# Latent attention's up-projections advanced piece by piece between halves of the convolution products, on a ring of five prepared and two raw weight tiles

## The chip, the cores and the metric

The kernel runs on one core of one Trainium2 chip. The metric is device time in microseconds (us) of one execution. TensorE (PE) multiplies matrices, with its weight loads (PEld) shown apart; VectorE (DVE), ScalarE (ACT) and GpSimd (POOL) work on tiles; SyncE (SP) issues DMA transfers. Each engine runs its own instructions in a fixed order and waits on semaphores for the others.

## The reference

Two blocks follow one another on 528 (16 meta and 512 real) and then 512 tokens of width 1024, all in float32. Block 1, one layer, computes

```
u, q, k, v, g_ssm, g_att = split(rmsnorm(h) @ w_in)
mixed = sigmoid(g_ssm) * (s5_mixer(u) @ w_ssm_out) + sigmoid(g_att) * (diff_attention(q, k, v) @ w_att_out)
h = h + mixed @ w_o
h = h + conv_glu_ffn(rmsnorm(h))
```

Block 2, two layers, projects a normed input to four branches, joins them with `w_out` and adds a normed result:

```
(a_val, a_glu, a_gate, b_q, b_f, b_i, b_gate, c_xbc, c_dt, c_z, d_cq, d_ckv, d_kr, d_gate) = split(rms_norm(x) @ w_in)
y_a = conformer_conv_branch(...)     # 31 taps along the tokens, layer norm, product
y_b = hgrn2_branch(...)              # gated recurrence in chunks of 64
y_c = ssd_branch(c_xbc, ...)         # 4 taps along the tokens, state space scan in chunks
y_d = mla_branch(d_cq, d_ckv, ...)   # latent attention
x = x + rms_norm(concat(y_a, y_b, y_c, y_d) @ w_out)
```

The latent attention `mla_branch` is what the change moves. From a normed query latent of 256 and a key-value latent of 128 columns it makes, by up-projections, the queries (64 plain and 32 rotated columns for each of 4 heads), the keys and the values:

```
q = (rms_norm(cq) @ qb_w);  q_rope = q_rope * cos + swapped(q_rope) * sin
k_nope, v = split(rms_norm(ckv) @ kvb_w)
o = softmax(mask(q k^T * 96 ** -0.5)) v        # 4 blocks of 128 queries x 4 heads
return o * silu(gate)
```

## The kernel before

**Products.** Every float32 product is made of three products of rounded parts, hi x hi, lo x hi and hi x lo (lines 466 to 468 of `mm3`), so a weight tile exists as `wh` (rounded) and `wl` (the rest). A product of one output tile of 128 columns over 1024 inputs and 512 tokens is 8 x 3 = 24 matmuls in one PSUM bank. PSUM has three banks for products (`pj`), two each for `sA` and `sB` (small products, scores, transposes) and one `so` (attention output). A product tile of a given bank can start only when the last result in that bank was read.

**Weights.** 197 tiles of 128 x 1024 stream from one tensor. `_fetch` (line 424 on) loads a raw tile `wr` by SP's queue, ScalarE copies it to `wh` (line 439), copies minus `wh` to `wl` (line 441), and GpSimd issues a DMA that adds the raw weights into `wl` (line 442). The first four tiles take `wl` from a VectorE subtraction instead (line 444). `weights(key)` hands out the next tile and keeps four fetched; the rings hold three raw and four prepared tiles.

**Order.** The code of block 2 is written as generators ("tasks"): `pump()` advances each task by one step, and `fm()`, the function for one product tile, pumps in the middle of its product and behind it, so a task's small products stand between halves of large ones. The tile framework's scheduler then sets each engine's order. In a layer of block 2 the products run b_f, b_q, kvm (the key-value latent and two small groups), d_cq (the query latent), b_i, a_glu and a_val; the gated recurrence (`hgrn_task`, its products at lines 345 and 1723) and, from the first a_val product on (read by VectorE's line 2273), the conformer convolution (`conf_conv`, 31 taps by line 1505 on VectorE) run beside them. Then `mla_proj` (line 2078) is called in one go: two query products, the rope products `pr` and `px` with VectorE's line 2098 (cos) and 2099 (sin) reading them, the key products, the value products (lines 2119 to 2121). It pumps the other tasks five times between its parts. Behind it come the six `c_xbc` products with `ssd_conv` between them, then c_z and the gates. The attention itself, `mla_attend`, is a task of 19 steps (score, line 2141; transposes, line 492; output, line 2169) and a closing part: gate multiplication by GpSimd, transposes, and the branch's parts 6 and 7 of the joining product `out2`.

**The end of a layer.** `out2` makes 8 output tiles, five over 512 tokens and three over two halves of 256; then a norm, the residual, and `lead` (lines 2358 to 2361): the first products of the next layer, of which the first weight tiles are held until all are done.

**Small pool.** 70 units of 128 x 528 serve all intermediate tiles; `S5_STARTS` sets at which pump count each of three groups of S5 work begins.

The pieces that the steps below follow:

```
w0 = self.weights(("sm", (l, 0)))
w1 = self.weights(("sm", (l, 1)))
self.spawn(self.mla_attend(l, *self.mla_proj(w0, w1)))
for g in range(2):
    for i in (g, 2 + g, 4 + g):
        self.xbc[i] = self.ssd_conv(l, i, self.fm(l, "c_xbc", i))
```

Of the kernel before, what the change touches and what calls it, by code (L numbers as in the profile page):

```python
# [8 lines left out]
F32 = mybir.dt.float32  # L9
F32R = mybir.dt.float32r  # L10
I32 = mybir.dt.int32
AF = mybir.ActivationFunctionType
ALU = mybir.AluOpType
# [6 lines left out]
GW = 1024  # L20
# [13 lines left out]
class Layout:  # L34
    def __init__(self):
        self.off = {}
        self.n = 0
# [273 lines left out]


class Build:
    NU = 70
    S5_STARTS = (8, 16, 24)
    HP = 300
    GLU_AT = 9

    def __init__(self, ctx, tc, ap, dbg=None):
        self.tc = tc  # L320
        self.nc = nc = tc.nc
        self.ap = ap
        self.dbg = dbg or {}
        self.vl, self.cl = layouts()
        ec = ctx.enter_context
        self.cp = ec(tc.tile_pool(name="cp", bufs=1))
        self.up = ec(tc.tile_pool(name="up", bufs=1))
        self.wp = ec(tc.tile_pool(name="wp", bufs=4))
        self.sp = ec(tc.tile_pool(name="sp", bufs=4))
        self.dp = ec(tc.tile_pool(name="dp", bufs=1, space=bass.MemoryType.DRAM))  # L330
        self.pp = ec(tc.tile_pool(name="pp", bufs=1, space=bass.MemoryType.PSUM))
        self.free_units = list(range(self.NU))
        self.owner = {}
        self.nid = 0
        self.worder = weight_order()
        self.wq = []
        self.tasks = []
        self.wnext = 0
# [81 lines left out]
    def _fetch(self, ahead=HP):  # L420
        nc = self.nc
        i = self.wnext
        self.wnext += 1
        kind, a = self.worder[i]
        n = GW
        if kind == "dn":
            n = (a[1] - a[0]) * 128
        elif kind == "pw" or kind == "sm" and a[1] == 0:
            n = 512
        with self.tc.high_priority(offset=ahead):  # L430
            raw = self.wp.tile([128, GW], F32, tag="wr", name=self.uid("wr"), bufs=3)
            h = self.wp.tile([128, GW], F32R, tag="wh", name=self.uid("wh"))
            l = self.wp.tile([128, GW], F32R, tag="wl", name=self.uid("wl"))
            cs = [slice(0, n)] if i else [slice(0, 512), slice(512, GW)]
            for c in cs:
                nc.sync.dma_start(out=raw[:, c], in_=self.ap["wst"][i, :, c])
            acc = self.lacc(i, kind, a)
            for c in cs:
                nc.scalar.activation(out=h[:, c], in_=raw[:, c], func=AF.Copy)  # L439
                if acc:  # L440
                    nc.scalar.activation(out=l[:, c], in_=h.bitcast(F32)[:, c], func=AF.Copy, scale=-1.0)  # L441
                    nc.gpsimd.dma_start(out=l[:, c], in_=self.ap["wst"][i, :, c], accum_op=ALU.add)  # L442
                else:
                    nc.vector.tensor_tensor(out=l[:, c], in0=raw[:, c], in1=h.bitcast(F32)[:, c], op=ALU.subtract)
        self.wq.append((self.worder[i], h, l))

# [1 line left out]
        return i >= 4  # L448

    def weights(self, key):  # L450
        while len(self.wq) < 4 and self.wnext < len(self.worder):
            self._fetch()
        k, h, l = self.wq.pop(0)
        assert k == key, (k, key)
        return h, l
# [794 lines left out]
    def block1(self):  # L1250
# [17 lines left out]
        def tick():  # L1268
            self.step += 1
            if self.step in self.S5_STARTS:  # L1270
                self.spawn(s5[self.S5_STARTS.index(self.step) + 1])
            self.pump()
# [802 lines left out]
            yield  # L2075
        self.free(*cq)

    def mla_proj(self, w0, w1):
        nc = self.nc
        V, G = nc.vector, nc.gpsimd  # L2080
        mm = nc.tensor.matmul
        SC = 96.0 ** -0.5
        ks, xk, xq = self.mks, self.xk, self.xq
        qs = [self.unit(F32, "mq") for _ in range(4)]
        for t in range(2):
            p = self.pj()
            self.mm3(p, w0[0], w0[1], t * 128, 128, 2, xq, slice(0, S), kstep=256)
            for hh in range(2):
                nc.scalar.activation(out=qs[t * 2 + hh][:64, :S], in_=p[hh * 64:hh * 64 + 64], func=AF.Copy, scale=SC)
            self.pump()  # L2090
        pr = self.pj()
        self.mm3(pr, w1[0], w1[1], 0, 128, 2, xq, slice(0, S))
        px = self.pj()
        self.mm3(px, w1[0], w1[1], 256, 128, 2, xq, slice(0, S))
        for x in xq:
            self.free(*x)
        ro, t = self.unit(), self.unit()
        V.tensor_tensor(out=ro[:, :S], in0=pr, in1=self.cosT, op=ALU.mult)  # L2098
        V.tensor_tensor(out=t[:, :S], in0=px, in1=self.sinT, op=ALU.mult)
        G.tensor_tensor(out=ro[:, :S], in0=ro[:, :S], in1=t[:, :S], op=ALU.add)  # L2100
        for h in range(4):
            nc.scalar.activation(out=qs[h][64:96, :S], in_=ro[h * 32:h * 32 + 32, :S], func=AF.Copy, scale=SC)
        self.free(ro, t)
        self.pump()
        for t in range(2):
            p = self.pj()
            self.mm3(p, w1[0], w1[1], 512 + t * 128, 128, 1, [xk], slice(0, S))
            nc.scalar.activation(out=ks[t * 2][:64, :S], in_=p[0:64], func=AF.Copy)
            nc.scalar.activation(out=ks[t * 2 + 1][:64, :S], in_=p[64:128], func=AF.Copy)
        self.pump()  # L2110
        vt = []
        for t in range(2):
            p = self.pj()
            for u in range(2):
                j = t * 2 + u
                o = p[:, u * 256:u * 256 + 256]
                sl = slice(j * 128, j * 128 + 128)
                wh, wl = w1[0][:, 768:1024], w1[1][:, 768:1024]
                mm(out=o, lhsT=xk[0][:, sl], rhs=wh, start=True, stop=False)
                mm(out=o, lhsT=xk[0][:, sl], rhs=wl, start=False, stop=False)  # L2120
                mm(out=o, lhsT=xk[1][:, sl], rhs=wh, start=False, stop=True)
            v = self.unit(F32, "mv")
            nc.scalar.activation(out=v[:, :S], in_=p, func=AF.Copy)
            vt.append(v)
        self.free(*xk)
        self.pump()
        return qs, ks, vt

    def mla_attend(self, l, qs, ks, vt):
        nc = self.nc  # L2130
# [73 lines left out]
    def layer(self, l):  # L2204
        nc = self.nc
# [71 lines left out]
                self.spawn(self.conf_conv(l, ths))  # L2277
            self.pump()
        self.spawn(self.conf_rest(l))
        w0 = self.weights(("sm", (l, 0)))  # L2280
        w1 = self.weights(("sm", (l, 1)))
        self.spawn(self.mla_attend(l, *self.mla_proj(w0, w1)))
        for g in range(2):
            for i in (g, 2 + g, 4 + g):
                self.xbc[i] = self.ssd_conv(l, i, self.fm(l, "c_xbc", i))
# [65 lines left out]
        for hs in H2:  # L2351
            for a in range(2):
                for k in range(8):
                    xh, xl = self.xn[k]
                    c = slice(k * 128, k * 128 + 128)
# [112 lines left out]
```

## Time and profile before

| | |
|---|---|
| median of 3 runs | 1389.48 us (1389.32 to 1390.44) |
| profiled execution | 1390.1 us, span 1388.3 us |
| PE busy | 1337.1 us, 96% |
| PEld, DVE, ACT, POOL busy | 87%, 58%, 56%, 34% |
| mean granted clock of TensorE | 0.982 of full speed |
| weights and other reads | 209.33 MB, 154 GB/s over the span |

The table is of one execution. Block 1 ends near 800 us; layer 0 of block 2 runs from there to about 1065 us, the turn from layer 0 to layer 1 lies between 1065 and 1112 us, and layer 1 ends the span. A stretch in which PE is busy all the time at granted clock 1.00 can't give time without fewer matmuls; a stretch with idle PE or a lower clock can. So the views of waits and of single stretches say more here than the shares of the span.

### The profile page before, as it was taken

What the parts mean: (1) busy time and instruction counts of PE and PEld (TensorE: products, weight loads), DVE (VectorE), ACT (ScalarE), POOL (GpSimd) and SP (SyncE); (2) the same over time, 40 slices, a digit from 0 to 9 for tenths busy, and PEclk for the clock granted to TensorE, in tenths of its full rate; (3) what the DMA queues carried; (4) which work ended last, traced back from release to release, by engine and by line L of the source; (5) the groups of instructions that cost most, each with busy time, mean ns of one, the idle gap of its engine ahead of it and who ended that gap; (6) DMA issues with size and microseconds to landing.
All of it is one profiled execution on the core that took longest, in us unless ns stands there. A gap on an engine that the chain in (4) does not pass through costs nothing.

```text
span 1388.3 us, 22901 instructions
## 1 busy us (share of the span) xinstructions
PE 1337.1 (96%) x8778; PEld 1201.4 (87%) x8778; DVE 805.0 (58%) x1951; ACT 777.9 (56%) x1217; POOL 471.5 (34%) x557
## 2 busy tenths in 40 slices
PE   8899999999999999999999989899998799899998
PEld 8898898999999988998898888779987798689986
DVE  8969776423533322332233485998633696998623
ACT  7565555654555443444445856665657666664653
POOL 4557731113332221221124443632212453632210
PEclk9999999999999999999999999999999889999999
DMA  8855555598888888888887956464468456474483
GB/s 271 219 120 115 116 118 130 128 227 185 182 195 185 186 187 192 185 186 191 186 180 159 208 118 153 106 150 107 96 138 202 101 127 145 91 164 102 92 175 91
DMA packets 72254, 215.54 MB, mean 155 GB/s; under 512 B 10705, under 2 KB 17361, under 8 KB 72145
## 3 DMA queue, kind: packets, MB, share of 16 engines
q0 software_dynamic: 27648, 98.58, 42.7%
q1 hardware_dynamic: 43488, 113.80, 25.3%
q10 hardware_dynamic: 1008, 1.70, 0.4%
q8 instruction: 69, 1.13, 0.3%
q14 instruction: 41, 0.33, 0.1%
HBM read 209.33 MB, written 4.72 MB: 154 GB/s over the span
## 4 chain that ended last, share of the span: by engine, by line
PE 78%; DVE 14%; ACT 1%; issue 1%; DMA 1%; POOL 0%; DVEq 0%; ACTq 0%
PE pj L466 17%; PE pj L468 17%; PE pj L467 17%; DVE cc L1505 3%; PE pj L1482 3%; PE pj L1481 3%; PE pj L1483 3%; PE sB L492 2%; PE sB L2141 1%; PE so L2169 1%; PE pj L2326 1%; PE pj L2324 1%; PE pj L2325 1%; DMA wl<-in_wst 1%; PE sB L1174 1%
## 5 line engine op out<-in xcount | busy, mean ns | idle before, releaser
L466 PE MATMUL pj<-xh,wh 128*128 128x512 f32 (+4 forms) x1700 | 556.4, 328 | 7.4 <-DVE u L2098 4.0
L467 PE MATMUL pj<-xl,wh 128*128 128x512 f32 (+4 forms) x1700 | 554.0, 326 | 0.0
L468 PE MATMUL pj<-xh,wl 128*128 128x512 f32 (+4 forms) x1700 | 554.0, 326 | 0.0
L439 ACT ACTIVATE wh<-wr 128x1024 fp32r<-128x1024 f32 (+2 forms) x197 | 203.8, 1036 | 353.1 <-PE pj L467 298.0
L442 POOL DMA_DIRECT2D wl<-in_wst x192 | 167.6, 873 | 560.2 <-ACT wl L441 544.8
L466 PEld LDWEIGHTS pj<-xh,wh 128*128 128x128 f32 x1700 | 321.9, 189 | 37.2 <-DVE u L2098 4.9
L467 PEld LDWEIGHTS pj<-xl,wh 128*128 128x128 f32 x1700 | 321.8, 189 | 26.6 <-issue 0.2
L468 PEld LDWEIGHTS pj<-xh,wl 128*128 128x128 f32 x1700 | 321.4, 189 | 26.9 <-issue 0.4
L441 ACT ACTIVATE wl<-wh 128x1024 fp32r<-128x1024 f32 (+2 forms) x192 | 198.6, 1036 | 2.7
L1481 PE MATMUL pj<-wh,xh 128*128 128x256 f32 x384 | 114.5, 298 | 3.2 <-DVE u L1595 3.1
L1482 PE MATMUL pj<-wl,xh 128*128 128x256 f32 x384 | 112.6, 293 | 4.1 <-DMA wl<-in_wst 4.1
L1483 PE MATMUL pj<-wh,xl 128*128 128x256 f32 x384 | 112.6, 293 | 0.0
L1481 PEld LDWEIGHTS pj<-wh,xh 128*128 128x128 f32 x384 | 75.5, 197 | 6.0 <-issue 5.8
L1482 PEld LDWEIGHTS pj<-wl,xh 128*128 128x128 f32 x384 | 75.3, 196 | 5.9 <-DMA wl<-in_wst 4.4
L1483 PEld LDWEIGHTS pj<-wh,xl 128*128 128x128 f32 x384 | 75.4, 196 | 1.0 <-issue 1.0
L1505 DVE SCALAR_TENSOR_TENSOR cc<-u,aw,cc 128x496 f32<-128x496 f32 (+17 forms) x84 | 73.2, 876 | 0.3
L1405 DVE TENSOR_TENSOR hT<-hT,pj 128x512 f32<-128x512 f32 x24 | 16.4, 687 | 88.3 <-PE pj L468 88.3
L1384 DVE TENSOR_TENSOR u<-pj,nsR 128x258 f32<-128x258 f32 (+1 forms) x44 | 18.6, 425 | 76.2 <-PE pj L468 68.9
L1390 DVE TENSOR_TENSOR u<-u,pj 128x512 f32<-128x512 f32 x22 | 15.2, 689 | 64.8 <-PE pj L468 60.4
L1512 POOL TENSOR_TENSOR ce<-ce,u 128x489 f32<-128x489 f32 (+7 forms) x32 | 47.4, 1482 | 10.7 <-ACT u L1511 9.6
L529 POOL TENSOR_TENSOR nsA<-nsA,u 128x514 f32<-128x514 f32 (+3 forms) x23 | 29.5, 1281 | 48.5 <-ACT u L528 36.5
L488 DVE SCALAR_TENSOR_TENSOR xl<-hT,vec,xh 128x256 fp32r<-128x256 f32 (+3 forms) x40 | 28.3, 723 | 18.8 <-ACT xh L487 18.8
(626 smaller groups left out, 2356.8 us busy)
## 6 DMA issues: line engine op xcount, KB each, us to landing
wr<-in_wst SPq DMA_DIRECT2D x183, 512.0 KB, 3.9
wl<-in_wst POOLq DMA_DIRECT2D x180, 512.0 KB, 6.0
hT<-in_xT SPq DMA_DIRECT2D x16, 264.0 KB, 5.7
wr<-in_wst SPq DMA_DIRECT2D x8, 384.0 KB, 3.1
wl<-in_wst POOLq DMA_DIRECT2D x8, 384.0 KB, 5.4
wr<-in_wst SPq DMA_DIRECT2D x6, 256.0 KB, 4.6
UD<-us SPq DMA_DIRECT2D x4, 264.0 KB, 6.9
U<-UD SPq DMA_DIRECT2D x16, 66.0 KB, 5.5
```

Of the source, the lines that this page charges most:

```text
L439: nc.scalar.activation(out=h[:, c], in_=raw[:, c], func=AF.Copy)
L441: nc.scalar.activation(out=l[:, c], in_=h.bitcast(F32)[:, c], func=AF.Copy, scale=-1.0)
L442: nc.gpsimd.dma_start(out=l[:, c], in_=self.ap["wst"][i, :, c], accum_op=ALU.add)
L466: mm(out=out, lhsT=a, rhs=xh[:, sl], start=k == 0, stop=False)
L467: mm(out=out, lhsT=a, rhs=xl[:, sl], start=False, stop=False)
L468: mm(out=out, lhsT=b, rhs=xh[:, sl], start=False, stop=k == nk - 1)
L529: eng.tensor_tensor(out=st["A"][:, hs], in0=st["A"][:, hs], in1=s[:, hs], op=ALU.add)
L1481: mm(out=o, lhsT=xh[:, sl], rhs=h, start=k == 0, stop=False)
L1482: mm(out=o, lhsT=xh[:, sl], rhs=lo, start=False, stop=False)
L1483: mm(out=o, lhsT=xl[:, sl], rhs=h, start=False, stop=k == 7)
L1505: V.scalar_tensor_tensor(out=c[:, o:S], in0=th[:, :S - o], scalar=aw[:, i, 30 - o:31 - o], in1=c[:, o:S], op0=ALU.mult, op1=ALU.add)
L1512: G.tensor_tensor(out=e[:, k:S], in0=e[:, k:S], in1=t[:, :S - k], op=ALU.add)
```

## The change

Four edits. (1) The pool of units shrinks from 70 to 68, and the third S5 group starts at count 28 instead of 24. (2) The prepared ring grows from four to five tiles, the raw ring shrinks from three to two, and five tiles are kept fetched. (3) `_fetch` makes `wl` from the raw tile by itself, before `wh`, and issues the adding DMA before `wh` is made. (4) `mla_proj` becomes a generator that fetches its own weights and yields eight times; a new task `mla_task` runs it and then the attention, and is put first among the tasks, so its parts now stand between halves of the `c_xbc` products.

```diff
-    NU = 70
-    S5_STARTS = (8, 16, 24)
+    NU = 68
+    S5_STARTS = (8, 16, 28)
...
-        self.wp = ec(tc.tile_pool(name="wp", bufs=4))
+        self.wp = ec(tc.tile_pool(name="wp", bufs=5))
...
-            raw = self.wp.tile([128, GW], F32, tag="wr", name=self.uid("wr"), bufs=3)
+            raw = self.wp.tile([128, GW], F32, tag="wr", name=self.uid("wr"), bufs=2)
...
             for c in cs:
+                if acc:
+                    nc.scalar.activation(out=l[:, c], in_=raw[:, c], func=AF.Copy, scale=-1.0)
+                    nc.gpsimd.dma_start(out=l[:, c], in_=self.ap["wst"][i, :, c], accum_op=ALU.add)
                 nc.scalar.activation(out=h[:, c], in_=raw[:, c], func=AF.Copy)
-                if acc:
-                    nc.scalar.activation(out=l[:, c], in_=h.bitcast(F32)[:, c], func=AF.Copy, scale=-1.0)
-                    nc.gpsimd.dma_start(out=l[:, c], in_=self.ap["wst"][i, :, c], accum_op=ALU.add)
-                else:
+                if not acc:
                     nc.vector.tensor_tensor(out=l[:, c], in0=raw[:, c], in1=h.bitcast(F32)[:, c], op=ALU.subtract)
...
-        while len(self.wq) < 4 and self.wnext < len(self.worder):
+        while len(self.wq) < 5 and self.wnext < len(self.worder):
...
-    def mla_proj(self, w0, w1):
+    def mla_proj(self, l):
...
+        w0, w1 = (self.weights(("sm", (l, i))) for i in range(2))
...
-            self.pump()
+            yield
         pr = self.pj()
         self.mm3(pr, w1[0], w1[1], 0, 128, 2, xq, slice(0, S))
+        yield
         px = self.pj()
...
+    def mla_task(self, l):
+        qkv = yield from self.mla_proj(l)
+        yield from self.mla_attend(l, *qkv)
...
-        w0 = self.weights(("sm", (l, 0)))
-        w1 = self.weights(("sm", (l, 1)))
-        self.spawn(self.mla_attend(l, *self.mla_proj(w0, w1)))
+        self.tasks.insert(0, self.mla_task(l))
+        self.pump()
```

By the change the rope reads of VectorE are lines 2100 and 2101, the score is line 2149, the output line 2177, the value products lines 2121 to 2123, and the copies and the adding DMA of `_fetch` are lines 442 (`wh`), 440 (`wl`) and 441.

**First place: PE in layer 0, the up-projections.** Before, `pj_9511` and `pj_9518` are the rope products, `pj_9539` and `pj_9545` the keys, `pj_9589` the first values, and `pj_9616` the first `c_xbc` product. Left-out rows are the other matmuls of the same tiles.

```order
L466 MATMUL pj_9511<-xh_9049,wh_9317 128x512
...
L466 MATMUL pj_9518<-xh_9049,wh_9317 128x512
...
L1791 MATMUL sA_9494<-u_9041,u_9466 128x128 x2
...
L466 MATMUL pj_9539<-xh_8851,wh_9317 128x512
...
L466 MATMUL pj_9545<-xh_8851,wh_9317 128x512
...
L2119 MATMUL pj_9589<-wh_9317,xh_8851 128x256
...
L466 MATMUL pj_9616<-xh_8015,wh_9385 128x512
```

In the changed kernel `pj_9559` and `pj_9591` are the rope products, `pj_9666` and `pj_9702` the keys, and `pj_9578` and `pj_9689` are `c_xbc` products.

```order
L466 MATMUL pj_9559<-xh_9056,wh_9231 128x512
...
L466 MATMUL pj_9578<-xh_8022,wh_9392 128x512
...
L466 MATMUL pj_9591<-xh_9056,wh_9231 128x512
...
L466 MATMUL pj_9578<-xh_8036,wh_9392 128x512
...
L466 MATMUL pj_9666<-xh_8858,wh_9231 128x512
...
L1912 MATMUL sA_9674<-bd_8830,s_8827 128x512
L466 MATMUL pj_9689<-xh_8022,wh_9447 128x512
...
L466 MATMUL pj_9702<-xh_8858,wh_9231 128x512
```

Before, the rope products stand side by side and the keys follow 6 matmuls behind; now 19 matmuls of a `c_xbc` product stand between the two rope products, its last 5 between the second rope product and the first key product, and 20 of the next `c_xbc` product between the two key products.

**Second place: ScalarE at the turn from layer 0 to layer 1.** Line 498 and 499 make the last part of the norm factors; the tiles `wr_11469`, `wr_11476` and `wr_11706` are the first three weights behind `lead`. Before:

```order
L499 ACTIVATE nsR_11158<-nsR_11158 128x256
L439 ACTIVATE wh_11470<-wr_11469 128x1024
L439 ACTIVATE wh_11477<-wr_11476 128x1024
L439 ACTIVATE wh_11707<-wr_11706 128x1024
L498 ACTIVATE nsR_11158<-sB_11634,eps_129 128x256
L441 ACTIVATE wl_11471<-wh_11470 128x1024
L441 ACTIVATE wl_11478<-wh_11477 128x1024
L441 ACTIVATE wl_11708<-wh_11707 128x1024
L499 ACTIVATE nsR_11158<-nsR_11158 128x256
```

In the changed kernel the first of the three was prepared earlier; the second and third are `wr_11476` and `wr_11483`, and `wr_11713` is the fourth.

```order
L499 ACTIVATE nsR_11165<-nsR_11165 128x256
L442 ACTIVATE wh_11477<-wr_11476 128x1024
L440 ACTIVATE wl_11478<-wr_11476 128x1024
L442 ACTIVATE wh_11484<-wr_11483 128x1024
L440 ACTIVATE wl_11485<-wr_11483 128x1024
L498 ACTIVATE nsR_11165<-sB_11641,eps_129 128x256
L499 ACTIVATE nsR_11165<-nsR_11165 128x256
L440 ACTIVATE wl_11715<-wr_11713 128x1024
```

Six copies of weights stand ahead of the last norm factors before, four in the changed kernel.

**Third place: ScalarE in the first 35 us.** `wr_169` and `wr_176` are the first two weights whose `wl` is made by an adding DMA, line 710 is a sine with its table load, line 498 begins the norm factors. Before:

```order
L439 ACTIVATE wh_170<-wr_169 128x1024
L441 ACTIVATE wl_171<-wh_170 128x1024
L439 ACTIVATE wh_177<-wr_176 128x1024
L441 ACTIVATE wl_178<-wh_177 128x1024
L710 ACT_TABLE_LOAD
L710 ACTIVATE s_cs<-s_cs 128x32
L402 ACT_TABLE_LOAD
```

In the changed kernel:

```order
L710 ACT_TABLE_LOAD
L710 ACTIVATE s_cs<-s_cs 128x32
L402 ACT_TABLE_LOAD
L440 ACTIVATE wl_171<-wr_169 128x1024
L442 ACTIVATE wh_170<-wr_169 128x1024
L440 ACTIVATE wl_178<-wr_176 128x1024
L442 ACTIVATE wh_177<-wr_176 128x1024
L498 ACTIVATE nsR_134<-pj_151,eps_129 128x176
```

The two weights' copies moved from ahead of the sine and its two table loads to behind them.

## Rows read from the trace of the kernel before

**Rows 1.** The page: busy us of each engine (share of the span) x instructions.

```profile
PE 1337.1 (96%) x8778; PEld 1201.4 (87%) x8778; DVE 805.0 (58%) x1951; ACT 777.9 (56%) x1217; POOL 471.5 (34%) x557
```

**Rows 2.** Stretches of 40 us; the columns are in the fence's first line.

```profile
core 0: us, PE busy (x) PEld busy (x) DVE busy (x) ACT busy (x) POOL busy (x), PEclk, DMA share, GB/s
240.00:280.00 40.00, 40.00 (x310) 37.52 (x309) 19.81 (x64) 26.37 (x45) 4.52 (x7) 1.00 0.64 146
880.00:920.00 40.00, 35.74 (x185) 28.68 (x186) 39.70 (x74) 26.81 (x43) 21.23 (x16) 0.96 0.54 120
1080.00:1120.00 40.00, 32.76 (x229) 30.71 (x228) 28.66 (x64) 25.67 (x45) 18.68 (x27) 0.87 0.44 106
1200.00:1240.00 40.00, 36.45 (x169) 29.15 (x168) 39.67 (x82) 29.07 (x48) 18.21 (x14) 0.91 0.64 134
```

**Rows 3.** PE's waits from 30 us on: waiting line, releaser, total, times, longest.

```profile
PE sB L345 <- DVE u L1662: 6.3, 2, 3.5
PE pj L1482 <- DMA wl<-in_wst: 4.1, 1, 4.1
PE pj L466 <- DVE u L2098: 4.0, 2, 2.0
...
PE sB L1723 <- DVE hD L1727: 3.7, 2, 1.9
PE pj L1481 <- DVE u L1595: 3.1, 1, 3.1
...
PE sA L901 <- DVE s L863: 2.2, 1, 2.2
PE pj L2119 <- DVE u L2099: 2.0, 2, 1.0
```

**Rows 4.** PE's timeline in layer 1: start, duration, engine, line, operation, tiles.

```profile
1210.97 0.63 PE L468 MATMUL pj<-xh,wl 128*128 128x512 f32 x1
1211.40 0.63 PE L466 MATMUL pj<-xh,wh 128*128 128x512 f32 x1
...
1214.31 0.39 PE L466 MATMUL pj<-xh,wh 128*128 128x512 f32 x1
1214.54 0.39 PE L467 MATMUL pj<-xl,wh 128*128 128x512 f32 x1
```

**Rows 5.** VectorE's timeline in layer 0, from a convolution's start to the rope read.

```profile
863.40 0.69 DVE L2273 SCALAR_TENSOR_TENSOR u<-u,pj 128x512 f32<-128x512 f32 x1 [3.44 <-PE pj L468]
...
888.41 0.73 DVE L1505 SCALAR_TENSOR_TENSOR cc<-u,aw,cc 128x499 f32<-128x499 f32 x1
...
895.04 0.68 DVE L2098 TENSOR_TENSOR u<-pj,cosT 128x512 f32<-128x512 f32 x1
```

**Rows 6.** ScalarE's timeline at the turn from layer 0 to 1.

```profile
1097.73 2.96 ACT L439 ACTIVATE wh<-wr 128x1024 fp32r<-128x1024 f32 x3 [7.24 <-PE pj L2360]
...
1103.79 0.40 ACT L499 ACTIVATE nsR<-nsR 128x256 f32<-128x256 f32 x1
```

**Rows 7.** The page's DMA issues: operation, count, KB each, us to landing.

```profile
wl<-in_wst POOLq DMA_DIRECT2D x180, 512.0 KB, 6.0
```

**Rows 8.** ScalarE's timeline in the first 30 us.

```profile
21.28 1.06 ACT L441 ACTIVATE wl<-wh 128x1024 fp32r<-128x1024 f32 x1
...
25.21 1.28 ACT L710 ACT_TABLE_LOAD   x1
...
27.12 1.28 ACT L402 ACT_TABLE_LOAD   x1
```

**Rows 9.** PE's timeline at the first product behind the norm.

```profile
33.12 0.39 PE L466 MATMUL pj<-xh,wh 128*128 128x272 f32 x1 [1.47 <-DVE us L638]
```

**Rows 10.** VectorE's timeline: the maximum of an attention score tile.

```profile
997.89 0.69 DVE L2144 TENSOR_REDUCE s<-sB 128x1 f32<-128x512 f32 x1
```

**Rows 11.** ScalarE's timeline: the exponential of the same score tile.

```profile
998.62 0.69 ACT L2146 ACTIVATE u<-sB,s 128x512 f32<-128x512 f32 x1 [3.67 <-DVE s L2144]
```

**Rows 12.** GpSimd's timeline: the attention branch's closing gate multiplication, layer 0.

```profile
1020.97 1.63 POOL L2195 TENSOR_TENSOR yd<-yd,g 128x512 f32<-128x512 f32 x1
```

More of the change, by code (lines that the diff above doesn't have):

```diff
@@ L2103, in mla_proj @@
         self.free(ro, t)
-        self.pump()
+        yield
         for t in range(2):
@@ L2109, in mla_proj @@
             nc.scalar.activation(out=ks[t * 2 + 1][:64, :S], in_=p[64:128], func=AF.Copy)
-        self.pump()
+            yield
         vt = []
@@ L2124, in mla_proj @@
             vt.append(v)
+            if t == 0:
+                yield
         self.free(*xk)
-        self.pump()
+        yield
         return qs, ks, vt
+    def mla_task(self, l):
+        qkv = yield from self.mla_proj(l)
+        yield from self.mla_attend(l, *qkv)
     def mla_attend(self, l, qs, ks, vt):
```

## The prediction, made before the changed kernel was run

> **What bounds the kernel now.** I read the busy times first. PE is busy for 1337.1 us, 96% of the span [rows 1]; no matmul is taken away, so what the change can gain is the 51 us in which PE stands, and what the lower clock costs around them. Then stretches: in the long middle of block 1 PE is busy 40.00 of 40 us at clock 1.00; around 900, 1100 and 1220 us it is busy 35.74, 32.76 and 36.45 of 40 at 0.96, 0.87 and 0.91 [rows 2]. So only block 2 and the start can move. Third, PE's waits by releaser [rows 3]: in both layers PE waits for the two rope reads (4.0 and 2.0 us in two times each), for VectorE in the gated recurrence (6.3 and 3.7), and at the turn between the layers for norm factors (3.1) and for a weight's low part (4.1). VectorE is full where the rope waits lie: 39.70 and 39.67 of 40 us [rows 2]. These waits are paid twice, since the clock falls behind them. In layer 1 a 512-column matmul starts 0.43 us after the one before it at 1210.97 and 0.23 us after it at 1214.31 [rows 4]; these are the 1.2 and the 2.4 GHz level. A mean clock of 0.91 over 40 us is 7.2 us at half speed, which costs 7.2 x (1 - 0.23 / 0.43) = 3.3 us; 0.96 is 3.2 us and costs 1.5.
>
> **Middle of layer 0.** The change takes no work from VectorE; it moves the readers of its results further back. Before, four product tiles follow one another with no long product between them, on three banks: the second key product needs the bank that line 2098 reads, the first value product the bank of line 2099. That goes: 2.0 + 1.0 us. The recurrence's wait for line 1727 goes too (1.9 of the 3.7), since 21 long matmuls now stand ahead of it, and with these waits the 1.5 us of low clock: 6.4 us in all. What comes late next is again VectorE. In the trace the way from the convolution's first input at 863.40 to the cos read at 895.04 takes 31.6 us [rows 5]. In the changed order I counted the operations between the same two, a tap of 0.73 [rows 5] and the others by their kind: about 31.6 us without disturbance against 28.7 before, that is 10% less than the trace shows. With the same slowing the cos read ends near 901 and the sin read 5.6 x 1.1 us of work later plus its own place, near 905.4. PE, without the old waits, reaches the first key product near 903 and the next `c_xbc` product, which needs the sin read's bank, near 904.1. So one wait of 1.3 us is left; bounds are 0 (VectorE undisturbed) and 4 (the slowing a third stronger, both reads late, and a low clock behind). I take 2, near the computed one with a little clock. Net: -4.4.
>
> **Middle of layer 1.** The same pieces, with the larger cost of clock: 2.0 + 1.0 + 1.8 + 3.3 = 8.1 us go, and I leave 2.6 for the new wait, VectorE being as full: -5.5.
>
> **Turn between the layers.** With five prepared tiles the first of the three weights behind the held ones is ready before these are released. ScalarE, which before started three copies at 1097.73 and ended the norm factors at 1104.19 after six [rows 6], makes four copies of about 1.03 us, then the factors: 1097.7 + 4.1 + 0.7 = 1102.5. VectorE's reads of the first products and so PE's 3.1 us wait end 1.7 us earlier. The second low part is issued near 1100.7 and lands after 6.0 us [rows 7] near 1106.7; PE now needs it near 1104.8. The wait of 4.1 thus falls to about 2, at worst 2.6, which I take: -1.5. The first score product of layer 1 stands 37 matmuls of 0.12 us further back, so 1.0 of its 2.8 us (6.3 less 3.5) go, and 0.8 of low clock. Sum: 1.7 + 1.5 + 1.0 + 0.8 = 5.0. Bounds: 1.7 (the low part lands as late as before) to 8 (both waits and their clock gone).
>
> **Start of layer 0.** The first score product stands 10 short matmuls later (1.2 of its 3.5 us go), but a recurrence product now stands 3 instead of 12 matmuls behind its forerunner; I take 0.7 back: -0.5, between -1.5 and +1.
>
> **Start of the kernel.** Here the change costs. With two raw tiles the fifth weight's raw tile can be loaded only when VectorE has made the third weight's low part, which itself stands later in its order, so the scheduler put the sine ahead of the copies. Before, the low part of the fifth weight was written at 21.28, ahead of the first of the two table loads at 25.21; the second ends at 28.40 [rows 8]. Now that copy runs from 28.4 to 29.4, GpSimd issues the addition in some 0.9, and it lands 6.0 later, near 36.3. PE started the product that needs it at 33.12, after a 1.47 us wait for VectorE [rows 9]. So PE comes 3 us later there. Behind it a wait of 2.2 for VectorE's line 863 [rows 3] takes some of that up, but VectorE itself slips by about 1.5, since its reads with the norm factors stand behind the same copies. I take +2; bounds are 0 (all taken up) and +4.
>
> Two pages move this one term. The Trainium skill's page "DMA: Bandwidth & Descriptors", section "Anatomy of one DMA — SWDGE (gpsimd) path", gives about 2.0 us plus the bytes over 436 GB/s for a transfer issued by GpSimd, so by estimate 3.2 us for 512 KB; then the low part would land near 33.5, in time, and the start would cost nothing. The median of 180 such transfers here is 6.0 [rows 7]; they read their target as well, and the measurement decides. The Trainium skill's page "ScalarE: Activation LUTs", section "What ACT_TABLE_LOAD costs", counts 1.28 us for a load and 1.38 more for a drain with each switch, 5.3 for two, which would put the copies 2 us later and the term near +4. The loads' 1.28 agrees with the row, the drain doesn't show: 25.21 to 28.40 holds both loads and a wait of the sine for its input [rows 8].
>
> **Ends of the layers.** The attention starts some four pumps later and now runs into `out2`. Its last scores stand 6 matmuls (1.4 us) apart in the changed order, where before 20 or more stood between. A score tile takes 0.69 for its maximum and 0.69 for its exponential [rows 10, 11], with the score's matmul and the hand-overs some 2.6 us before its transposes; the scheduled pieces between cover this but for about 1 us per layer. Then, in layer 0, the first three `out2` tiles stand half done for the branch's last two parts: 5 matmuls (1.2 us) lie between the last output and its transposes' result, and the way is a scaling of 0.4, the gate multiplication of 1.63 [rows 12], transposes, and two copies of 0.7, 3.9 us. So 2.7 us are new, where before 30 matmuls covered them, and 1 for the scores; with a little rounding down 3.5, between 1 and 8. In layer 1 28 matmuls cover the same way; +1, between 0 and 5.
>
> **What costs nothing.** The two units less: the least number of free units in block 2 rises, since the latents' pieces are spread. The S5 group four counts later is hidden: its output lay some 25 us ahead of its reader. The order of `wh` and `wl` in `_fetch` is nothing in the middle of block 1, where a slot's way from release to landed low part, 2.1 + 0.9 + 6.0 = 9 us by the same rows, faces 16.8 us of products with four tiles. If that cover were gone, PE's 40.00 of 40 would fall at once.
>
> **Sum.** -0.5 - 4.4 - 5.0 - 5.5 + 2 + 3.5 + 1 = -8.9 us. The profiled run took 1390.1, a span of 1388.3 and 1.8 around it, 0.6 above the median of 1389.5. Forecast for the median: 1380.6.
>
> **Rivals.** (a) VectorE is the true bound of both middles: it is full at 39.7 of 40, nothing is taken from it, and each wait removed comes back at the next bank or recurrence product. For it speaks that every wait there names VectorE; against it that from 960 on VectorE has room, while PE still has products to put in. Both middles then give 0: 1389.5 + 1.0 = 1390.5. (b) Slower: the late attention is the bound of both layers' ends. Its steps are a chain through four engines with only two `sB` banks, shared with the branches' transposes; if each of the last six steps of a layer waits 1.5 us instead of hiding, and the last parts come behind weight transfers in GpSimd's queue, an end costs 10 us instead of 3.5 and 1: +15.5, 1396. It decides from 13.4 us for both ends on, where the gain is used up. For it speaks the 1.4 us spacing against 2.6 us of a score; against it that three steps are in flight. (c) The ring changes nothing and its start costs 4: the turn's wait is for the low part of the third tile instead, so -5.0 becomes 0 and +2 becomes +4: 1387.6. For it speaks that the seven tiles in flight stay seven.
>
> **How the numbers follow.** Forecast 0.64, with its own range 1373 to 1387 (the bounds of the four larger terms, half used); (a) 0.15, (b) 0.13, (c) 0.08. Below lies the case in which every named wait goes and nothing comes back, 6.4 + 8.1 + 8 us less 2 at the ends, about 1369. The range 1370 to 1391 leaves out most of (b) and the edge of that case, some 0.2. A change of 0.2%, 2.8 us, is about what a measurement can tell. Faster by more: 0.62 of the forecast, 0.05 of (a), 0.04 of (c), 0.71. Slower: 0.11 of (b), 0.02 of the others, 0.13. Within: 0.16.
>
> **What would show it.** Right: PE's list of waits without the keys' and values' waits for the rope reads, clock near 1.00 at 1200 to 1240, the norm factors at the turn over a microsecond earlier, a new weight wait near 34 us, a new wait for transposes in layer 0's `out2`. Wrong: PE idle in the middles as before under other releasers (a), waits of over 1 us at several scores near the layers' ends (b), the turn's weight wait unchanged (c), or any idle PE between 240 and 800 us.

## The result and the profile after

The changed kernel is slower: 1400.19 us median of 4 runs (1396.73 to 1402.00) against 1389.40 (1387.68 to 1390.44), a ratio of 1.0075 with a 95% interval of 1.0062 to 1.0087, so 8.6 to 12.1 us. The forecast was 1380.6 and the range ended at 1391. The profiled execution took 1396.73 us, a span of 1395.0, and is the fastest of the four; the two traces compared below are thus 6.7 us apart in their spans, where the medians are 10.8 apart.

The page's busy times after:

```profile
PE 1336.9 (96%) x8778; PEld 1196.8 (86%) x8778; DVE 800.2 (57%) x1951; ACT 772.9 (55%) x1221; POOL 463.4 (33%) x557
```

PE does the same work in nearly the same busy time as in [rows 1]. The loss is therefore looked for in idle time and clock, stretch by stretch. The windows of the changed kernel, with the columns in the first line:

```profile
core 0: us, PE busy (x) PEld busy (x) DVE busy (x) ACT busy (x) POOL busy (x), PEclk, DMA share, GB/s
0.00:40.00 40.00, 33.30 (x241) 32.47 (x242) 32.34 (x136) 26.18 (x43) 12.24 (x28) 0.96 0.68 208
880.00:920.00 40.00, 37.05 (x200) 30.24 (x200) 39.60 (x72) 22.61 (x34) 20.14 (x16) 0.96 0.47 105
1000.00:1040.00 40.00, 37.93 (x199) 29.45 (x198) 17.17 (x36) 20.63 (x36) 6.02 (x6) 1.00 0.58 132
1080.00:1120.00 40.00, 34.81 (x242) 32.17 (x242) 27.55 (x72) 25.85 (x50) 14.13 (x21) 0.92 0.47 111
1200.00:1240.00 40.00, 34.85 (x184) 27.31 (x183) 39.35 (x77) 27.92 (x43) 21.03 (x17) 1.00 0.49 106
1320.00:1360.00 40.00, 35.79 (x185) 27.43 (x184) 14.38 (x28) 17.71 (x29) 4.75 (x5) 1.00 0.49 108
```

In the middles the kernel did as it was meant to in one respect: the clock from 1200 on is 1.00 instead of 0.91 [rows 2], yet PE is busy 34.85 of 40 instead of 36.45. At 880 it gained 1.3 us. New are idle PE in the first 40 us (33.30; before 36.30 at clock 1.00) and at both layers' ends, 1000 to 1040 and 1320 to 1360, where the kernel before had 40.00 of 40. The same three stretches of the kernel before:

```profile
0.00:40.00 40.00, 36.30 (x274) 35.47 (x275) 34.88 (x148) 28.85 (x47) 15.46 (x31) 1.00 0.89 276
1000.00:1040.00 40.00, 40.00 (x211) 33.41 (x210) 14.30 (x26) 21.62 (x32) 6.54 (x7) 1.00 0.61 138
1320.00:1360.00 40.00, 40.00 (x202) 33.15 (x201) 11.53 (x20) 23.39 (x34) 6.52 (x7) 1.00 0.75 157
```

PE's waits after, total, times and longest:

```profile
PE sB L345 <- DVE s L1868: 5.9, 1, 5.9
PE pj L624 <- DVE wl L444: 4.9, 2, 3.8
PE pj L2365 <- ACT xh L487: 3.0, 1, 3.0
PE sA L2394 <- DMA wl<-in_wst: 2.9, 1, 2.9
PE sB L492 <- DVE s L506: 2.7, 1, 2.7
PE sB L1198 <- ACT u L498: 2.6, 1, 2.6
...
PE sB L345 <- DVE u L1662: 2.1, 1, 2.1
...
PE pj L466 <- DVE u L1595: 1.8, 4, 0.7
...
PE pj L1481 <- DVE u L1595: 1.6, 1, 1.6
...
PE pj L1482 <- DMA wl<-in_wst: 1.6, 1, 1.6
PE pj L466 <- DVE u L2101: 1.5, 1, 1.5
PE pj L466 <- ACT mk L2111: 1.5, 2, 1.2
```

Against [rows 3], the waits for the cos and the sin read, 6.0 us, shrank to one of 1.5, and the turn's pair (3.1 and 4.1) to 1.6 and 1.6. In their place stand waits for the evacuation of other products (line 1595), for copies of keys (`mk`), for a weight at the very end (2.9) and for a weight at the very start (3.8 of the 4.9; the other wait there was 0.9 before and is 1.0 now). The first recurrence product of layer 1, which waited 2.75 us before, now waits 5.9. In the two middles, 840 to 1000 and 1160 to 1315 us, all of PE's waits together were 6.0 and 5.9 us before and are 5.1 and 5.9 now.

To see where time is lost and won, I summed the columns of all matmuls in order of time and noted when each execution reaches the share that the kernel before reaches at a given time. Inside a layer the shift also moves when small products are put off. Each row is one execution: e5 and e6 below give PE the same order of matmuls up to about 860 us and still differ by 3.7 us at 282, so differences of a few us between rows say little, and the profiled execution of e6 is 2.7 us faster than its median.

| kernel before at | 41 | 282 | 763 | 1004 | 1044 | 1084 | 1124 | 1326 | 1366 |
|---|---|---|---|---|---|---|---|---|---|
| changed kernel | +4.1 | +10.7 | +10.5 | +0.1 | +8.7 | +6.8 | +0.9 | -2.0 | +6.8 |
| edits 1 to 3 (e2) | +3.8 | +12.2 | +11.9 | +6.4 | +6.4 | +5.6 | +0.8 | +1.3 | +0.3 |
| edit 4 alone (e1) | 0.0 | +1.4 | +1.3 | -2.9 | +6.9 | +7.4 | +6.7 | +4.2 | +9.9 |
| edits 1 to 3, start put right (e6) | +3.6 | -0.2 | -0.6 | -5.4 | -5.4 | -6.8 | -13.2 | -15.2 | -14.9 |

Three things are to be read: some 10 us are lost before 282, in block 1; the turn (1084 to 1124) gives 6 back; and each layer's end (1004 to 1044, 1326 to 1366) takes back 9 us that edit 4 seemed to have won inside the layer.

**The start.** VectorE's third low part (line 444) before, then in the changed kernel, each with start and duration, and PE's wait for it:

```profile
18.09 1.21 DVE L444 TENSOR_TENSOR wl<-wr,wh 128x1024 fp32r<-128x1024 f32 x1
```

```profile
23.46 1.22 DVE L444 TENSOR_TENSOR wl<-wr,wh 128x1024 fp32r<-128x1024 f32 x1
```

```profile
24.73 1.03 PE L624 MATMUL pj<-xh,wl 128*128 128x264 f32 x3 [3.82 <-DVE wl L444]
```

PE stood for 3.82 us. ScalarE meanwhile had loaded the sine's table and waited for its input, so the fifth weight's copy came at 28.5 instead of 21.28 [rows 8], as forecast (28.4):

```profile
27.00 0.23 ACT L710 ACTIVATE s_cs<-s_cs 128x32 f32<-128x32 f32 x1 [5.65 <-DVE s_cs L665]
...
28.54 1.06 ACT L440 ACTIVATE wl<-wr 128x1024 fp32r<-128x1024 f32 x1
```

The copy that the forecast priced came later than before but made no wait of its own; PE was already late by the wait for the third weight.

**The turn.** PE's two waits, 3.1 and 4.1 before [rows 3], are shorter, as forecast. The first of them before, then ScalarE's first copy and the two waits in the changed kernel:

```profile
1105.06 1.15 PE L1481 MATMUL pj<-wh,xh 128*128 128x256 f32 x2 [3.13 <-DVE u L1595]
```

```profile
1105.45 1.06 ACT L442 ACTIVATE wh<-wr 128x1024 fp32r<-128x1024 f32 x1 [6.87 <-PE pj L2367]
```

```profile
1111.03 0.36 PE L1481 MATMUL pj<-wh,xh 128*128 128x256 f32 x1 [1.62 <-DVE u L1595]
...
1114.36 0.38 PE L1482 MATMUL pj<-wl,xh 128*128 128x256 f32 x1 [1.55 <-DMA wl<-in_wst]
```

From ScalarE's first copy to the end of PE's first wait it took 7.33 us before (1097.73 [rows 6] to 1105.06) and takes 5.58 now (1105.45 to 1111.03): 1.75 us less, where 1.7 was forecast.

**The end of layer 1.** The last read of the attention's output bank, the matmul that frees a weight, ScalarE's next weight copy, and PE's last waits:

```profile
1343.40 0.42 DVE L2184 TENSOR_TENSOR yd<-so,s 128x256 f32<-128x256 f32 x1 [4.86 <-PE so L2177]
```

```profile
1348.04 0.39 PE L2394 MATMUL so<-wl,xh 128*128 128x512 f32 x1
```

```profile
1348.47 1.06 ACT L440 ACTIVATE wl<-wr 128x1024 fp32r<-128x1024 f32 x1 [10.77 <-PE so L2394]
```

```profile
1352.05 0.50 PE L2393 MATMUL pj<-wh,xh 128*128 128x512 f32 x1 [0.79 <-ACT xh L487]
...
1357.06 0.50 PE L2394 MATMUL sA<-wl,xh 128*128 128x512 f32 x1 [2.88 <-DMA wl<-in_wst]
```

ScalarE was free for 10.77 us before that copy, which makes the sixth joining weight in the slot of the first. The first joining weight is used by four product tiles, and the fourth of them lies in the bank `so`, in which the attention makes its outputs. So it could start only behind the read at 1343.40, PE made it after the other three, and the slot came free behind its matmul at 1348.04. The sixth weight's low part was then late by 2.88 us for PE. This second cost of a late attention, a bank and with it a weight's slot, was in no step of the forecast.

### The profile page after: what moved, and what is told of

It reads as the page before. It is cut to its first block, busy times and chain, and to the rows that moved or that the text cites. A ratio compares the mean times of both kernels' runs of the same rounds, so it can differ in the third digit from the quotient of the medians.

```text
span 1395.0 us, 22910 instructions
## 1 busy us (share of the span) xinstructions
PE 1336.9 (96%) x8778; PEld 1196.8 (86%) x8778; DVE 800.2 (57%) x1951; ACT 772.9 (55%) x1221; POOL 463.4 (33%) x557
## 4 chain that ended last, share of the span: by engine, by line
PE 69%; DVE 19%; ACT 5%; issue 4%; DMA 2%; POOL 1%; SPq 0%; DVEq 0%; ACTq 0%; POOLq 0%
PE pj L466 16%; PE pj L467 16%; PE pj L468 15%; DVE cc L1505 4%; PE pj L1482 2%; PE pj L1483 2%; PE pj L1481 2%; PE sB L492 2%; ACT wl L440 1%; DVE hZ L1682 1%; PE sB L2149 1%; DVE xbc L1848 1%; PE pj L2331 1%; PE sB L1174 1%; PE pj L2332 1%
## 5 line engine op out<-in xcount | busy, mean ns | idle before, releaser
L440 ACT ACTIVATE wl<-wr 128x1024 fp32r<-128x1024 f32 (+2 forms) x192 | 197.3, 1027 | 28.9 <-PE so L2394 11.8
L1481 PE MATMUL pj<-wh,xh 128*128 128x256 f32 x384 | 110.2, 287 | 1.6 <-DVE u L1595 1.6
L1505 DVE SCALAR_TENSOR_TENSOR cc<-u,aw,cc 128x511 f32<-128x511 f32 (+20 forms) x84 | 76.4, 909 | 1.0
L492 PE MATMUL sB<-cst,u 128*128 128x128 f32 x192 | 33.7, 276 | 2.8 <-DVE s L506 2.7
```

What stands on the lines that cost most here:

```text
L440: nc.scalar.activation(out=l[:, c], in_=raw[:, c], func=AF.Copy, scale=-1.0)
L492: self.nc.tensor.transpose(p[:, j * 128:j * 128 + 128], src(j), self.ident[:kk, :kk])
L1481: mm(out=o, lhsT=xh[:, sl], rhs=h, start=k == 0, stop=False)
L1505: V.scalar_tensor_tensor(out=c[:, o:S], in0=th[:, :S - o], scalar=aw[:, i, 30 - o:31 - o], in1=c[:, o:S], op0=ALU.mult, op1=ALU.add)
```

## The experiments

All were timed against runs of the kernel before on the same chip; ratios have 95% intervals.

**e1, edit 4 alone.** The rings, the fetch order, the units and the S5 starts of before, with `mla_task` and the generator `mla_proj` of the change.

> Edit 4 alone: the up-projections advanced piece by piece, on the old rings (four prepared, three raw), 70 units, S5 starts and fetch order of before. Theory A (the loss lies in the first 265 us and comes from the rings and the S5 start; the new attention order gains in layer 0 and gives it back at both layers' ends): first product behind the norm at 33 us as before, no change up to 800 us, the two rope waits gone, new waits at the layers' ends; in the changed kernel block 2 without the turn gained about -3 in layer 0 with its end and lost about +6 in layer 1, so 1389 to 1394. Rival B (the new attention order is itself the loss, the start is taken up later): 1396 to 1400. Rival C (the new attention order gains what was forecast): 1380 to 1385.

1398.9 us, ratio 1.0068 (1.0056 to 1.0081): rival B. Three of its waits on PE:

```profile
908.71 0.50 PE L466 MATMUL pj<-xh,wh 128*128 128x512 f32 x1 [1.18 <-DVE u L2101]
...
919.93 0.79 PE L466 MATMUL pj<-xh,wh 128*128 128x512 f32 x1 [2.94 <-DVE u L1595]
...
1035.03 0.66 PE L492 MATMUL sB<-cst,yd 128*128 128x128 f32 x4 [1.63 <-POOL yd L2203]
```

The rope waits of 6.0 us in two layers are replaced by one for the sin read (1.18) and one for the evacuation of a `c_xbc` product (2.94) in layer 0, and by 1.94 and 1.39 for the same two in layer 1; layer 0's end waits for the late attention's gate multiplication (1.63). My theory A, read off the changed kernel's row of the table above before this run, had put the loss into block 1; it was half wrong.

**e2, edits 1 to 3.** The kernel without `mla_task`.

> Edits 1 to 3 without 4: five prepared and two raw tiles, the new fetch order, 68 units and the third S5 group at 28, the up-projections in one go as before. Theory A: PE waits 3 to 4 us for the third weight's low part near 25 us, reaches the product behind the norm 5 us late, is about +10 at 300 us, and gains about 6 at the turn between the layers; middles of the layers as before: 1392 to 1396. Rival B: the start's delay is taken up before 300 us, the turn gains: 1383 to 1388.

1389.82 us, ratio 1.0003 (0.9994 to 1.0012). Neither expectation: the 12 us of block 1 are there, and block 2 wins all of them back, so what edits 1 to 3 lose and what they win cancel.

**e3, edit 1 alone.**

```diff
-    NU = 70
-    S5_STARTS = (8, 16, 24)
+    NU = 68
+    S5_STARTS = (8, 16, 28)
```

> Edit 1 alone: 68 units and the third S5 group at count 28 instead of 24. It tells the second half of the loss in the first 265 us (the changed kernel went from +4 at 200 us to +10.5 at 262 us): if it comes from the later S5 group, this kernel is +4 to +7, 1393 to 1396, with waits of small products between 180 and 240 us; if that half follows from the late start and the lower clock after it, this kernel is the kernel before, 1388 to 1391.

1383.26 us, ratio 0.9962 (0.9948 to 0.9975). A miss on both: 2 us were won in block 1 and the rest in block 2, in which there is no S5 work and two units fewer mean other buffers for the same tiles. PE's order differs from that of the kernel before from its 375th matmul on. Part of the gain can be placed: from 800 to 820 us this run moves ahead by 3.6 us, and so do all other runs with fewer units and the third S5 group at 28 (by 2.4 to 4.6), while e1 and e10, with 70 and 24, gain nothing there; PE's wait for the first recurrence product of layer 0 falls from 3.53 to 2.14 us. Which of the two numbers does it wasn't tried.

**e4, the changed kernel with three raw tiles.**

```diff
-    NU = 68
+    NU = 66
...
-            raw = self.wp.tile([128, GW], F32, tag="wr", name=self.uid("wr"), bufs=2)
+            raw = self.wp.tile([128, GW], F32, tag="wr", name=self.uid("wr"), bufs=3)
```

> The changed kernel with three raw tiles instead of two beside the five prepared ones (66 units instead of 68 pay for the space). Undoes only what put the sine ahead of the first copies. Theory A: the first product behind the norm at 33 us again, so at least the 5 us of the start come back: 1393 to 1396, and if the second half of the loss follows from the late start, 1388 to 1391. Rival (the raw ring is not the cause, the start's delay is taken up anyway): 1397 to 1402.

1405.37 us, ratio 1.0119 (1.0105 to 1.0133): slower still. It has its own late start (PE waits 4.94 us at 36.80 for the norm's results), so its time doesn't isolate the raw ring; 66 units changed the order too. It shows one thing: with three raw tiles the third weight's low part starts at 18.29 again, and PE's wait of 3.82 for it is gone.

**e5 and e6, the start put right by two edits at once,** in the changed kernel and in edits 1 to 3. The third and fourth raw weight go through spare units, which also makes their loads and copies two halves each, and four tiles are kept fetched for the first 40.

```diff
+            us = [self.unit(), self.unit()] if i in (2, 3) else []
+            raw = None if us else self.wp.tile([128, GW], F32, tag="wr", name=self.uid("wr"), bufs=2)
...
+        while len(self.wq) < (5 if self.wnext >= 40 else 4) and self.wnext < len(self.worder):
```

> The changed kernel with the start put right: the third and fourth weight go through spare units instead of the two raw tiles, and four instead of five tiles are kept fetched for the first 40 tiles, so that the first copies for adding DMAs stand ahead of the sine again. Theory D (the new rings cost about 10 us in block 1, all of it following from the late start, and win about as much in block 2; edit 4 costs about 10 beside that): PE reaches 300 us at most 2 us later than before, and the time is 1388 to 1392. Rival E (block 1 loses by another order of its small products that the rings bring about, whatever the start): 1395 to 1401.

> Edits 1 to 3 with the same start, without edit 4. Theory D: the 10 us that block 1 lost with the rings are back and the gain of block 2 stays: 1378 to 1382. Rival E: 1387 to 1391.

e5: 1392.48 us, 1.0020 (1.0011 to 1.0029). e6: 1377.02 us, 0.9915 (0.9901 to 0.9928). Both times are near theory D and far from E, though each is just outside its range (e5 0.5 us above, e6 1 below), and e5's trace is 3.3 us late at 282 where at most 2 was expected. Edits 1 to 3 with a good start are worth 12 us, of which edit 1 alone gave 5.3 (e3), and edit 4 costs 1.0020 - 0.9915, 14.6 us, on top of them.

**e7, a quicker attention,** and **e9**, the same in edits 1 to 3 as a control.

```diff
-        yield from self.mla_attend(l, *qkv)
+        for n, _ in enumerate(self.mla_attend(l, *qkv)):
+            if n % 3 != 2:
+                yield
```

> As the changed kernel with the start put right, but the attention takes three steps in two pumps, so it ends some six pumps earlier and out of the joining products. Theory F (what edit 4 loses is lost at the layers' ends): 4 to 7 us less than the run without this edit, no waits for attention transposes in the joining products. Rival G (it is lost in the middle, where VectorE is full and each wait returns at the next bank): within 2 us of it, or slower since more of the attention falls into the full stretch.

> Control for the quicker attention: edits 1 to 3 with the start put right, the up-projections in one go, and the attention taking three steps in two pumps. Theory F (the 12 us came from an attention that ends inside the joining products, which only edit 4 brings about): no change from the same kernel with slow attention, 1375 to 1380. Rival (a quicker attention gains by itself): 1366 to 1372.

e7: 1380.34 us, 0.9939 (0.9926 to 0.9952), 11.3 us less than e5. e9: 1376.47 us, 0.9917 (0.9904 to 0.9930), the same as e6. So an attention that ends earlier is worth 11 us with edit 4 and nothing without it: most of what edit 4 loses is the lateness it gives the attention. PE's busy time is 1333.1 us in both traces, so the 10.3 us between their spans are idle time: 5.9 went at the two ends (6.1 in e5, 0.25 in e7), about 4.5 elsewhere; that is more than theory F said, and not at the ends alone. What stays of edit 4 is 0.9939 - 0.9917, about 3 us.

**e8, edit 4 in layer 0 only.** In layer 1 the generator runs through at once, with a pump after each piece.

> As the changed kernel with the start put right, with the up-projections piece by piece in layer 0 only and in one go (eight pumps between) in layer 1. Splits edit 4 by layer: if its loss is even, 4 to 6 us less than with both layers; if it lies in layer 1 (the changed kernel was 6 us later over layer 1 than the kernel with the rings alone, 3 over layer 0), 6 to 8 less; if in layer 0, 0 to 3.

1383.99 us, 0.9965 (0.9951 to 0.9978): 7.6 us less than e5, 6.9 more than e6. The 7.6 fall into the range expected for a loss in layer 1, but the ranges were made for a loss of some 10 us; of the 14.6 measured it is half, so the loss is even over the layers to within the intervals.

**e10, edit 4 alone with the quicker attention** (e1 with the diff of e7).

> Edit 4 alone on the rings of before, with the quicker attention (three steps in two pumps). Theory F: most of the 10 us that edit 4 alone lost come back and nothing is won against the kernel before: 1388 to 1392. Rival (edit 4 wins in the middles what was forecast once the ends are clear): 1378 to 1383. If the loss has nothing to do with the ends on these rings: 1397 to 1400.

1394.42 us, 1.0043 (1.0027 to 1.0060). Only 3.5 of e1's 9.4 us come back. Between the expectations: on the old rings the waits of the middles remain (1.18, 2.92, 2.17 and 2.21 us for the sin read and line 1595), and edit 4 wins nothing. That the lateness of the attention is most of edit 4's loss thus holds on the rings with a good start, not on the old ones.

**e11 and e12, VectorE relieved.** Every second convolution tap on VectorE is left out in e6 and in e7.

```diff
+                if o % 2 == 0:
                     V.scalar_tensor_tensor(...)
```

> Edits 1 to 3 with the start put right, up-projections in one go, and every second of VectorE's 21 taps per convolution tile left out (about 15 us of VectorE's work per layer; the output is not the reference's). If a full VectorE makes the waits for the rope reads, they go (2.8 us in layer 0 in the same kernel with all taps) without edit 4, and the kernel is 4 to 10 us faster. If the waits are made by the order of the products and their banks, they stay near 3 us.

> The same taps left out in the changed kernel with the start put right and the quicker attention. Theory A (edit 4 has nothing to win in the middles beyond what VectorE's room decides): no faster than the kernel with the same taps left out and the up-projections in one go, 0 to 4 slower. Rival (edit 4 wins in the middles once VectorE has room): 2 to 6 faster than that kernel.

e11: 1368.71 us, 0.9857 (0.9845 to 0.9870). e12: 1373.36 us, 0.9898 (0.9884 to 0.9912). The wait of the first value product for the sin read in e6, then in e11, and the one wait for it in e7:

```profile
893.32 0.39 PE L2123 MATMUL pj<-wh,xh 128*128 128x256 f32 x1 [2.60 <-DVE u L2103]
```

```profile
891.56 0.39 PE L2124 MATMUL pj<-wh,xh 128*128 128x256 f32 x1 [0.62 <-DVE u L2104]
```

```profile
906.28 0.50 PE L470 MATMUL pj<-xh,wh 128*128 128x512 f32 x1 [1.50 <-DVE u L2105]
```

With VectorE relieved the wait falls from 2.60 to 0.62 with the products still side by side: in layer 0 a full VectorE makes it. A full VectorE alone isn't enough, though: in layer 1 of e6 VectorE is busy for 59.29 of 60 us (1170 to 1230), and no product waits for a rope read. With edit 4 the relieved kernel is 5.7 us slower, not faster. PE's idle time in the two middles (840 to 1000, 1160 to 1315) is nearly the same in both, 2.6 and 1.7 us in e11, 2.2 and 1.7 in e12, so edit 4 has next to nothing to win there. Where it loses the 5.7 isn't shown; the two profiled executions differ by 1.8 us only.

**e13 and e14, which of the two edits of e6 puts the start right.** e13 has the depth alone, e14 the spare units (with their halves) alone.

> Edits 1 to 3 with only the depth put right: four instead of five tiles kept fetched for the first 40 tiles, the third and fourth raw weight still through the two raw tiles. If the raw ring of two makes the late start (VectorE's low part of the third weight comes 5 us later), the time stays with edits 1 to 3, 1388 to 1392; if the depth makes it, 1376 to 1380.

> Edits 1 to 3 with only the raw ring put right: the third and fourth raw weight through spare units, five tiles kept fetched from the start. If the raw ring of two makes the late start, 1376 to 1381; if the depth makes it, 1388 to 1392; if both cost, between.

e13: 1395.18 us, 1.0044 (1.0031 to 1.0057). e14: 1377.70 us, 0.9917 (0.9904 to 0.9929). PE's first wait behind 16 us in e13, and in e14:

```profile
25.84 1.03 PE L624 MATMUL pj<-xh,wl 128*128 128x264 f32 x3 [3.84 <-DVE wl L444]
```

```profile
33.60 0.39 PE L470 MATMUL pj<-xh,wh 128*128 128x272 f32 x1 [1.99 <-DVE us L642]
```

The raw ring of two is the cause; the depth isn't. The depth alone is even slower than e2, by 5.7 us and above both expectations, which stays unexplained. That halving the loads has no part in it wasn't tried by itself, but in e4, with three raw tiles and whole loads, the wait at line 444 is gone too. Edits 1 to 3 with the spare units are 11.5 us faster than the kernel before and 1.0003 - 0.9917, 12 us, faster than e2; e6 and e9 are as fast.

## Why the prediction was wrong

Its steps, against the runs:

- **Start of the kernel, +2 with bounds 0 to 4: failed.** e2 against e14 says 12. The mechanism named (two raw tiles, a late third low part, the sine ahead of the copies) is the right one. The step that failed is what it was priced by: I followed the fifth weight's copy and its landing, and didn't price the third weight's own use, though the text says that it comes later. PE wanted it near 20.9 and got it at 24.7. That wait is 3.8 us. By 282 us it had become 10: idle PE up to there rose from 11.9 to 18.2, with new waits of 2.0, 2.6 and 2.7 us at 89, 184 and 226 us (two of 2.3 and 1.9 went), and the stretches of 40 us at a clock of 0.96 went from two to five, 1.6 us each (40 x 0.04). That the one wait brings on all the others isn't shown link by link; without it, in e6 and e14, the 10 are gone. The expectation that later waits take the delay up was the wrong way round.
- **Middles, -4.4 and -5.5: failed.** Rival (a) is what happened, as a mechanism. VectorE stayed full (39.60 and 39.35 of 40), and the waits came back at line 1595's bank, the key copies and the recurrence: 11.9 us in the two middles before, 11.0 after. In e7 and e9, with start and ends out of the way, edit 4 costs 3 us where the two steps together promised 9.9. With taps left out (e11, e12) it still costs. And in layer 1 the gain wasn't edit 4's to make: the rope waits there are gone with edit 1 alone (e3) and with edits 1 to 3 and a good start (e6, e9, e14). One reading was off as well: from a cos read that ends near 901, a sin read 5.6 x 1.1 us later ends near 907.2 and not 905.4 (measured, 6.18 us lie between the two), so the wait left would have been 3.1 and not 1.3.
- **Ends of the layers, +3.5 and +1: the mechanism right, the size not.** PE idles 2.1 and 4.2 us in the two windows that were full before, 6.3 against 4.5; but putting the attention forward gives 11.3. The forecast missed that the attention's output bank holds back a joining product and so its weight's slot, and that a late attention costs inside the layers too. It is rival (b) in kind, at 11 us and not at 20.
- **Turn, -5.0: the number right, one of its terms not.** The waits fell by 1.5 and 2.5, the shift by 5.9; in e6 by 6.4. ScalarE's way to the norm factors is shorter by 1.75 us, forecast 1.7; in e3, on the old rings, it is 7.33 us as before, in e6 5.57. But the first score product of layer 1, which was to lose 1.0 of its 2.8 us of wait, now waits 5.88 (5.85 in e6), and e3 moves ahead by 3.0 us in the same stretch without the rings, so not all of the 5.9 is theirs.
- **What wasn't seen.** Edit 1, costed at nothing, is worth 5.3 us alone (e3), mostly through another order in block 2. Why the order falls better stays open. Edits 1 to 3 with a good start win 12 us, of which the turn explains 6.

By the ratios the loss can be laid out as: edits 1 to 3 with a good start (e14) -11.5, the raw ring's start (e2 less e14) +12.0, edit 4 (the changed kernel less e2) +10.0, in all the 10.4 measured, to rounding. This is one way through the runs and no check of them, since each term begins where the last one ends: edit 4 costs 9.4 us on the old rings (e1), 10.0 on the new ones and 14.6 with a good start (e5 less e6). The first two terms nearly cancel, so the changed kernel shows edit 4's loss.

## What to carry to other kernels

Before a wait on a full engine is counted as won, ask what that engine finishes next: moving readers gives no work away, and the wait comes back at the next bank. When a task starts later, follow it to its last consumer: the banks that it still uses hold back products, and these hold weight slots. And when a ring shrinks, price the first use of every tile that passes through it while the kernel starts, not only the tile that the change of order points to.

## What the runs showed of the hardware

The cost of a stall at the start grew from 3.8 us of wait to 10 us of time at 282. Behind the wait at 24.73 three 264-column matmuls took 1.03 us together where they took 0.63 at 11.88, so the lower clock level came with it (the granted clock of the first 40 us is 0.96, before 1.00). The same block without the wait (e6, e14) was within 1 us of the kernel before at 282, although PE began its first product behind the norm 0.5 to 2.2 us late (33.60 and 35.31, before 33.12); the other runs with the start of e6 (e5, e7, e8, e9, e11, e12) were between 0.6 us early and 3.3 late there. Small delays were mostly taken up, the large one wasn't, and its size isn't fixed: in e13 the same wait of 3.84 us stood for 17 us at 282, in an execution 2.9 us slower than its median.
